# The seven-product form carried into w_down, with partial sums added up in DRAM

## The chip, the cores and the metric

The kernel runs on one core of one Trainium2 chip. The metric is device time in microseconds (us) from launch to end. The kernel before has a median of 2252.35 us over 3 runs (2251.71 to 2253.55). Everything is float32 at the input and output.

## What is computed

One layer of an encoder over 512 tokens and a model width of 2048: a norm, a combined projection into two groups of heads (dilated window attention and gated linear attention), an output projection with a residual, and then the part that matters here, a gated feed-forward block with a hidden width of 5632, and a last norm:

```python
h = rmsnorm(x, ffn_norm_w[l])
x = x + (jax.nn.silu(h @ w_gate[l]) * (h @ w_up[l])) @ w_down[l]
return rmsnorm(x, final_norm_w)
```

The change touches the last product, `@ w_down`: a 512 x 5632 matrix (called g below) times a 5632 x 2048 one, and what comes just before and after it.

## The kernel before, in words

**Precision.** Every large product is made of three matmuls. Each operand is split into a high part `hi` (rounded to the matmul type fp32r, a cast on ACT) and a low part `lo` (the rest, a subtraction on VectorE, DVE), and hi x hi, hi x lo and lo x hi are summed in PSUM.

**Memory.** There are 70 slots of [128, 512] called `a` (`s2`), 16 slots of [128, 1024] called `b` (`s4`) and the 8 PSUM banks `ps`. A slot given back goes to the end of a queue of free slots and is reused in that order; whoever writes it next waits for its last reader.

**Order.** The program is written in the order in which each engine executes: each engine takes its instructions in program order, and so do the queues of SP and POOL, from which transfers are issued. Work that should run beside matmuls is put between them by hand: `urgent` holds generators of which `run_urgent` executes one step at a time.

**w_gate and w_up** (`Feed`, lines 1059 to 1205). These already use a form with seven instead of eight block products for each pair of K-tiles (a K-tile is 128 rows of the contraction): both operands are cut into a 2 x 2 arrangement of blocks, sums of blocks are made on DVE, and seven products of 256 tokens are made. A piece is four K-tiles by 256 columns: a 512 KB load, `sums` (lines 1095 to 1097, DVE), `split` (1107 casts on ACT, 1112 subtractions on DVE), `products` (1137 to 1139, 42 matmuls of 256 columns). In turn i the program has the split of piece i+1 and the sums of piece i+2, then the products of piece i. After four pieces `evac` takes the sums out of PSUM, and every second time the gated result goes to DRAM as a tile `gd[j]` (line 1180), 256 hidden columns for all tokens. The operands made from x for this form come from `pair_operands` (lines 974 to 988).

**w_down** (lines 1209 to 1283). The 44 K-tiles of g are worked in three groups of K-tiles, 0 to 17, 18 to 35, 36 to 39, and a tail, 40 to 43. `g_load` and `g_split` bring g back from `gd` and split it. In each group, for each of four blocks c of 512 output columns, a job (`run_job`) goes through the K-tiles: for each, one half of a 512 KB load of w_down is split (`st.split`, lines 196 and 197), three halves ahead, and 4 x 3 matmuls of 512 columns follow (lines 293 to 295), one PSUM bank for each block of 128 tokens. At the end of a job `evac_down` adds the four banks, scaled by the row factor `rstd2`, to the residual tiles `x1` (line 1247), which POOL's queue has loaded from `xd` in DRAM at the end of w_up (line 1244).

**The tail** (`finish`, from line 1292). It goes token block by token block: for each of four blocks of 512 columns 12 matmuls (lines 1325 to 1327), the residual, the squares for the norm on ACT, a product with the norm's weight on DVE (line 1331). After the four blocks, `later` works out the factor of the last norm, scales (line 1311) and stores. The 16 halves of weights that the tail needs are split during the jobs of the third group, because there the lookahead grows by `4 * j.tail + i`.

Of the kernel before, what the change touches and what calls it, by code (L numbers as in the profile page):

```python
# [117 lines left out]
def layer(nc, tc, x, attn_norm_w, w_in, rel_table, gw_f, gb_f, gw_b, gb_b, gla_norm_w, w_out,  # L118
# [7 lines left out]
    with tc.manual_schedule(), \  # L126
# [136 lines left out]
        def run_job(j):  # L263
            if j.start:
                j.start()
            if j.limit:
                st.limit = j.limit
            banks = [ps.get() for _ in range(4)]
            per = len(j.kts) // j.n
            for i in range(j.n):  # L270
                if j.before:
                    j.before(i)
                st.load()
                st.split(j.first + i + AHEAD + (4 * j.tail + i if hasattr(j, "tail") else 0))
                _, _, wh, wl = st.halves[j.first + i]
                ks = j.kts[i * per:(i + 1) * per]
                for b in range(4):
                    for s_, k in enumerate(ks):
                        xh, xl = j.acts(k)
                        first = i == 0 and s_ == 0  # L280
                        last = i == j.n - 1 and s_ == per - 1
                        if j.kind == "A":
                            o = banks[b].t
                            c = slice(b * P, (b + 1) * P)
                            mm(o, wh.t[:, c], xh.t, start=first, stop=False)  # L285
                            mm(o, wh.t[:, c], xl.t, start=False, stop=False)  # L286
                            mm(o, wl.t[:, c], xh.t, start=False, stop=last)  # L287
                        else:
                            n = 512 // per
                            o = banks[b].t[:, 0:n]  # L290
                            c = slice(b * P, (b + 1) * P)
                            w = slice(s_ * n, (s_ + 1) * n)
                            mm(o, xh.t[:, c], wh.t[:, w], start=first, stop=False)  # L293
                            mm(o, xh.t[:, c], wl.t[:, w], start=False, stop=False)  # L294
                            mm(o, xl.t[:, c], wh.t[:, w], start=False, stop=last)  # L295
# [760 lines left out]
        n_out = len(jobs) - 1  # L1056


        class Feed:

            def __init__(self):
                self.units = [(w, j) for j in range(FF // 256) for w in (w_gate, w_up)]
                self.per = NP // 2
                self.seq = [(u, q) for u in range(len(self.units)) for q in range(self.per)]
                self.seq.insert(self.per + 1, self.seq.pop(self.per - 1))
                self.n = len(self.seq)
                self.raw, self.S, self.sets = {}, {}, {}  # L1070
                self.n_load = self.n_sums = 0

            def load(self):
                while self.n_load < self.n and len(self.raw) < 3 and s4.free:
                    u, q = self.seq[self.n_load]
                    w, j = self.units[u]
                    k = 4 * q
                    r = s4.get(F32, [P, 2, 4, P])
                    sp.dma_start(out=r.t.rearrange("p a b c -> p (a b c)").rearrange("p (k c) -> p k c", k=4),
                                 in_=w[k * P:(k + 4) * P, j * 256:(j + 1) * 256].rearrange("(k p) c -> p k c", p=P))  # L1080
                    self.raw[self.n_load] = r
                    self.n_load += 1

            def sums(self, i):


                if i != self.n_sums or i >= self.n:
                    return
                self.n_sums += 1
                if i not in self.raw:  # L1090
                    self.load()
                r = self.raw[i].t
                S = self.S[i] = s4.get(F32, [P, 2, 4, P])
                s_ = S.t
                dve.tensor_tensor(s_[:, :, 0:2], r[:, :, 1:3], r[:, :, 0:1].to_broadcast([P, 2, 2, P]), op=OP.add)  # L1095
                dve.tensor_tensor(s_[:, :, 2], s_[:, :, 0], r[:, :, 2], op=OP.add)
                dve.tensor_tensor(s_[:, :, 3], s_[:, :, 2], r[:, :, 3], op=OP.add)

            def split(self, i):
                if i >= self.n or i in self.sets:  # L1100
                    return
                r = self.raw[i]
                parts = [(r.t[:, :, 1:4], [P, 2, 3, P]), (self.S[i].t, [P, 2, 4, P])]
                his = []
                for src, shape in parts:
                    hi = s4.get(F32R, shape)
                    act.copy(hi.t, src)  # L1107
                    his.append(hi)
                out_ = []
                for (src, shape), hi in zip(parts, his):  # L1110
                    lo = s4.get(F32R, shape)
                    dve.tensor_tensor(lo.t, src, hi.f, op=OP.subtract)  # L1112
# [3 lines left out]
                self.load()  # L1116

            def products(self, i, banks):
                st_ = self.sets.pop(i)
# [109 lines left out]
        def down_start(q):  # L1229
            if q == 0:  # L1230
                g_load(0)
            if q == 1:
                st.until = None
                st.limit = 3
                st.load()
                g_load(1)
            if q == 2:
                g_split(0)
                st.split(down_first + 2)
            if q == 3:  # L1240
                for c in range(4):
                    x1[c] = [s2.get() for _ in range(4)]
                    for t in range(4):
                        pool.dma_start(out=x1[c][t].t, in_=xd[4 * c + t])

        def residual(c, t, bank):
            dve.scalar_tensor_tensor(x1[c][t].t, bank.t, rstd2[:, t:t + 1], x1[c][t].t, op0=OP.mult, op1=OP.add)  # L1247
# [8 lines left out]
        def before_down(h0, c, more):  # L1256
            def f(i):
                k = h0 + i
                if c == 0 and k % 2 == 0:
                    g_load(k // 2 + 2)  # L1260
                    g_split(k // 2 + 1)
                if more == LAST and c == 1 and i == 0:
                    g_split(FF // 256 - 1)
            return f

        def drop_g(k):
            put(*gT.pop(k))

        LAST = 40
        state["g"] = 0  # L1270
        st.until = len(st.pieces)
        down_first = len(st.halves)
        h0 = 0
        for h1 in (18, 36, LAST):
            for c in range(4):
                j = job("B", [piece512(w_down, c * 512, k) for k in range(h0, h1, 2)], list(range(h0, h1)),
                        lambda k: gT[k], evac_down(c), rate=1.0, before=before_down(h0, c, h1))
                if c == 3:
                    j.drop = drop_g
                if h1 == LAST:  # L1280
                    j.tail = c
            h0 = h1

        wf = []

# [8 lines left out]
        def finish():  # L1294

            first = len(st.halves)
            st.big = first
# [17 lines left out]
            def run():  # L1315
                for t in range(4):
                    ys = []
                    for c in range(4):
                        b = ps.get()
                        tok = slice(t * P, (t + 1) * P)  # L1320
                        for k in range(per):
                            st.split(first + c * per + k + 1)
                            _, _, wh, wl = st.halves[first + c * per + k]
                            xh, xl = gT[LAST + k]
                            mm(b.t, xh.t[:, tok], wh.t, start=k == 0, stop=False)  # L1325
                            mm(b.t, xh.t[:, tok], wl.t, start=False, stop=False)  # L1326
                            mm(b.t, xl.t[:, tok], wh.t, start=False, stop=k == per - 1)  # L1327
# [8 lines left out]

        run_last = finish()
        for n, j in enumerate(jobs):
            if getattr(j, "tail", None) == 0:
                start_tail()  # L1340
            run_job(j)
            if n == n_out:
                ff.run()
        drain()
        run_last()


# [25 lines left out]
```

## Time and profile before

| | |
|---|---|
| median of 3 runs | 2252.35 us |
| the profiled execution | 2252.81 us, of which the span from the first to the last instruction is 2251.0 |
| granted TensorE clock | 0.998 of full speed |
| TensorE busy | 2231.6 us, 99% |
| VectorE busy | 1453.2 us, 65% |
| ScalarE (ACT) busy | 900.2 us, 40% |
| data moved by transfers | 274 MB, 122 GB/s |

The page of the profile gives busy time by engine, the same in 40 slices of the span, the chain of work that ended last, and groups of instructions by line. In a group, `out<-in` names tiles without buffer numbers, then come the shapes, the count, the busy time in us, the mean of one in ns, and the idle time before them with what ended it. In a timeline the columns are the start, the length in us, the engine, the line and the operation, and in brackets the idle time of the engine before it and what released it. A matmul's length in the profile overlaps that of its neighbours, so two matmuls' distance is read from their starts. PE is TensorE, PEld its weight loads, SPq and POOLq the queues on which transfers are issued.

### The profile page before, as it was taken

What the parts mean: (1) busy time and instruction counts of PE and PEld (TensorE: products, weight loads), DVE (VectorE), ACT (ScalarE), POOL (GpSimd) and SP (SyncE); (2) the same over time, 40 slices, a digit from 0 to 9 for tenths busy, and PEclk for the clock granted to TensorE, in tenths of its full rate; (3) what the DMA queues carried; (4) which work ended last, traced back from release to release, by engine and by line L of the source; (5) the groups of instructions that cost most, each with busy time, mean ns of one, the idle gap of its engine ahead of it and who ended that gap; (6) DMA issues with size and microseconds to landing.
All of it is one profiled execution on the core that took longest, in us unless ns stands there. A gap on an engine that the chain in (4) does not pass through costs nothing.

```text
span 2251.0 us, 33982 instructions
## 1 busy us (share of the span) xinstructions
PE 2231.6 (99%) x13662; PEld 2001.6 (89%) x13662; DVE 1453.2 (65%) x2429; ACT 900.2 (40%) x1505; POOL 40.4 (2%) x79
## 2 busy tenths in 40 slices
PE   8999999999999999999999999999999999999998
PEld 7888887888888888999999999999999888888886
DVE  4366665744454356888888888888888623332356
ACT  5244454443454344433444344443444422322332
POOL 0000000000000100000000000000000100000000
PEclk9999999999999999999999999999999999999999
DMA  5524624332323432333333333433334942343312
GB/s 204 157 83 137 191 80 130 91 115 64 103 71 127 140 122 75 113 123 118 116 122 113 121 117 116 126 114 113 122 114 136 340 151 86 123 166 100 116 38 75
DMA packets 193358, 274.02 MB, mean 122 GB/s; under 512 B 13327, under 2 KB 129215, under 8 KB 193200
## 3 DMA queue, kind: packets, MB, share of 16 engines
q1 hardware_dynamic: 187584, 256.22, 36.2%
q0 software_dynamic: 4720, 14.58, 1.8%
q8 instruction: 107, 1.75, 0.3%
q10 hardware_dynamic: 896, 1.06, 0.1%
q14 instruction: 51, 0.42, 0.1%
HBM read 239.24 MB, written 19.99 MB: 115 GB/s over the span
## 4 chain that ended last, share of the span: by engine, by line
PE 97%; DVE 1%; ACT 1%; DMA 0%; issue 0%; ACTq 0%; SPq 0%
PE ps L1139 13%; PE ps L1137 13%; PE ps L1138 13%; PE ps L293 12%; PE ps L295 12%; PE ps L294 12%; PE ps L285 5%; PE ps L286 5%; PE ps L287 5%; PE ps L514 1%; PE ps L841 1%; PE ps L1326 1%; PE ps L1325 1%; PE ps L1327 1%; PE ps L554 1%; PE ps L553 1%
## 5 line engine op out<-in xcount | busy, mean ns | idle before, releaser
L1139 PE MATMUL ps<-a,b 128*128 128x256 f32 x2464 | 698.4, 283 | 2.9 <-DVE b L1112 2.9
L1137 PE MATMUL ps<-a,b 128*128 128x256 f32 x2464 | 698.1, 283 | 0.0
L1138 PE MATMUL ps<-a,b 128*128 128x256 f32 x2464 | 698.0, 283 | 0.0
L1107 ACT CAST b<-b 128x768 fp32r<-128x768 f32 x352 | 326.8, 942 | 406.5 <-DVE b L1112 253.5
L1139 PEld LDWEIGHTS ps<-a,b 128*128 128x128 f32 x2464 | 473.8, 192 | 3.8 <-DVE b L1112 3.8
L1138 PEld LDWEIGHTS ps<-a,b 128*128 128x128 f32 x2464 | 473.8, 192 | 0.0
L1137 PEld LDWEIGHTS ps<-a,b 128*128 128x128 f32 x2464 | 473.7, 192 | 0.0
L197 DVE TENSOR_TENSOR a<-b,a 128x512 fp32r<-128x512 f32 x420 | 279.5, 688 | 253.3 <-ACT a L196 253.1
L1112 DVE TENSOR_TENSOR b<-b,b 128x768 fp32r<-128x768 f32 x352 | 373.1, 1089 | 102.2 <-PE ps L1138 63.6
L293 PE MATMUL ps<-a,a 128*128 128x512 f32 x976 | 382.7, 392 | 0.0
L295 PE MATMUL ps<-a,a 128*128 128x512 f32 x976 | 380.0, 389 | 0.0
L294 PE MATMUL ps<-a,a 128*128 128x512 f32 x976 | 380.0, 389 | 0.0
L196 ACT CAST a<-b 128x512 fp32r<-128x512 f32 x420 | 249.2, 619 | 264.9 <-PE ps L295 239.5
L295 PEld LDWEIGHTS ps<-a,a 128*128 128x128 f32 x976 | 183.2, 188 | 38.5
L294 PEld LDWEIGHTS ps<-a,a 128*128 128x128 f32 x976 | 183.3, 188 | 37.2
L293 PEld LDWEIGHTS ps<-a,a 128*128 128x128 f32 x976 | 183.3, 188 | 37.1
L285 PE MATMUL ps<-a,a 128*128 128x512 f32 x416 | 167.8, 403 | 0.0
L286 PE MATMUL ps<-a,a 128*128 128x512 f32 x416 | 163.0, 392 | 0.0
L287 PE MATMUL ps<-a,a 128*128 128x512 f32 x416 | 162.7, 391 | 0.0
L1095 DVE TENSOR_TENSOR b<-b 128x512 f32<-128x512 f32 x176 | 120.4, 684 | 4.1 <-DMA b<-in_w_up_dram 4.1
L1247 DVE SCALAR_TENSOR_TENSOR a<-ps,small,a 128x512 f32<-128x512 f32 x64 | 45.5, 750 | 118.6 <-PE ps L295 107.5
L578 ACT CAST b<-ps 128x512 fp32r<-128x512 f32 x64 | 37.6, 587 | 144.8 <-PE ps L514 142.9
(196 smaller groups left out, 2312.1 us busy)
## 6 DMA issues: line engine op xcount, KB each, us to landing
b<-in_w_gate_dram SPq DMA_DIRECT2D x88, 512.0 KB, 3.5
b<-in_w_up_dram SPq DMA_DIRECT2D x88, 512.0 KB, 3.5
b<-in_w_down_dram SPq DMA_DIRECT2D x88, 512.0 KB, 4.9
b<-in_w_in_dram SPq DMA_DIRECT2D x96, 256.0 KB, 4.3
b<-in_w_in_dram SPq DMA_DIRECT2D x48, 512.0 KB, 4.1
b<-in_w_out_dram SPq DMA_DIRECT2D x32, 512.0 KB, 4.5
a<-a SPq DMA_DIRECT2D x96, 128.0 KB, 2.3
gd<-b SPq DMA_DIRECT2D x22, 512.0 KB, 2.7
```

Of the source, the lines that this page charges most:

```text
L197: dve.tensor_tensor(h[3].t, r, h[2].f, op=OP.subtract)
L285: mm(o, wh.t[:, c], xh.t, start=first, stop=False)
L286: mm(o, wh.t[:, c], xl.t, start=False, stop=False)
L287: mm(o, wl.t[:, c], xh.t, start=False, stop=last)
L293: mm(o, xh.t[:, c], wh.t[:, w], start=first, stop=False)
L294: mm(o, xh.t[:, c], wl.t[:, w], start=False, stop=False)
L295: mm(o, xl.t[:, c], wh.t[:, w], start=False, stop=last)
L1107: act.copy(hi.t, src)
L1112: dve.tensor_tensor(lo.t, src, hi.f, op=OP.subtract)
L1137: mm(o, wh, xh, start=head, stop=False, skip_group_check=True)
L1138: mm(o, wh, xl, start=False, stop=False, skip_group_check=True)
L1139: mm(o, wl, xh, start=False, stop=end, skip_group_check=True)
```

## The change

Of the 22 pairs of K-tiles in w_down, pairs 2 to 19 go over to the seven-product form. Pairs 0 and 1 stay plain and are worked first, pairs 20 and 21 remain the tail.

- `Feed` is divided: what loads, sums up and splits the weights goes into a class `Blocks`, from which `Feed` and a new class `Down` inherit. For w_gate and w_up nothing changes.
- `Down` works in three chunks of six pairs. In each chunk, for each block c of 512 columns, it goes through the six pairs: one 512 KB piece of w_down, its sums and splits, and seven products. Each product goes into a PSUM bank of its own, in two halves of 128 tokens, with the tokens' side as the stationary operand: 42 matmuls of 256 columns.
- `operands` is a generator that brings a pair of g back from `gd`, makes the sums and the splits, in four steps a pair; it waits for 2 free b slots and for 13 free a slots. `make(n)` executes n steps: two at the end of w_up, three before each K-tile of the plain jobs, two after each piece of `Down`.
- After the six pairs of a chunk the seven banks are copied to SBUF by ACT and sent to `md` in DRAM: on SP in the first chunk, on POOL's queue and added to what is there (`accum_op`) in the second and third. Four of the seven are copied within the last piece, three at the start of the next (`evac_late`).
- In the last chunk, `combine(c)` reads the seven sums and the residual tiles back and puts the result of a block together on DVE, seven sums and four scaled additions, spread over later pieces as `urgent` work. For the last block it is executed in the tail, before the first use of that block.
- The plain jobs no longer add to `x1`: ACT scales the bank, and POOL's queue adds it to `xd` in DRAM. `x1` is loaded by `combine`.
- The weights of the tail are split two halves at a time in the last four pieces, eight of the 16; the others in the tail, each just before its matmuls. The tail's other work is as before.

```diff
@@ run_job
-                st.split(j.first + i + AHEAD + (4 * j.tail + i if hasattr(j, "tail") else 0))
+                st.split(j.first + i + AHEAD)
@@ plain jobs
         def evac_down(c):
             def f(banks):
                 for t in range(4):
-                    residual(c, t, banks[t])
+                    y = s2.get()
+                    act.activation(y.t, banks[t].t, AF.Copy, scale=rstd2[:, t:t + 1])
+                    put(banks[t])
+                    pool.dma_start(out=xd[4 * c + t], in_=y.t, accum_op=OP.add)
+                    put(y)
             return f
+        def before_down(c):
             def f(i):
+                if c == 0 and i == 0:
+                    g_split(1)
+                dn.make(3)
+                if c == 3:
+                    dn.load()
+                    if i >= 1:
+                        dn.sums(i - 1)
+                    if i == 2:
+                        dn.split(0)
             return f
@@ class Down(Blocks)
+            def operands(self):
+                a, z = slice(0, 256), slice(256, 512)
+                tt = dve.tensor_tensor
+                for q in [q for ch in self.chunks for q in ch]:
+                    while len(s4.free) < 2:
+                        yield
+                    r = s4.get(F32, [P, 2, 512])
+                    sp.dma_start(out=r.t.rearrange("p f t -> p (f t)"), in_=gd[q])
+                    yield
+                    while len(s2.free) < 9 + 4:
+                        yield
+                    n1, f2 = r.t[:, 1], r.t[:, 0]
+                    t13, t24 = s2.get(), s2.get()
+                    tt(t13.t[:, a], n1[:, z], n1[:, a], op=OP.subtract)
+                    tt(t13.t[:, z], f2[:, z], n1[:, z], op=OP.add)
+                    tt(t24.t[:, a], f2[:, z], t13.t[:, a], op=OP.add)
+                    tt(t24.t[:, z], t24.t[:, a], f2[:, a], op=OP.subtract)
+                    yield
...
+                    for i, (src, hi, lo, hf) in enumerate(todo):
+                        if i == 0:
+                            act.activation(hi, src, AF.Copy, scale=-1.0)
+                            dve.scalar_tensor_tensor(lo, src, -1.0, hf, op0=OP.mult, op1=OP.subtract)
+                        else:
+                            act.copy(hi, src)
+                            tt(lo, src, hf, op=OP.subtract)
+                        if i:
+                            put((r, t13, t24)[i - 1])
+                        if i % 2:
+                            yield
...
+            def products(self, i):
...
+                prods = [(R(0), "B11"), (R(2), "B21"), (Z(2), "T2"), (Z(1), "T1"), (Z(0), "T3"), (Z(3), "B22"),
+                         (R(1), "T4")]
+                for n, ((wh, wl), x) in enumerate(prods):
...
+                    for h in range(2):
+                        o = self.banks[n].t[:, h * 256:(h + 1) * 256]
+                        t = slice(h * P, (h + 1) * P)
+                        mm(o, xh[:, t], wh, start=first and h == 0, stop=False, skip_group_check=True)
+                        mm(o, xh[:, t], wl, start=False, stop=False, skip_group_check=True)
+                        mm(o, xl[:, t], wh, start=False, stop=last, skip_group_check=True)
+                    if last:
+                        if n < 4:
+                            self.evac(ch, c, n, self.banks[n])
+                        else:
+                            self.late.append((ch, c, n, self.banks[n]))
...
+            def combine(self, c):
+                m = [s2.get(F32, [P, 2, 256]) for _ in range(7)]
+                for n in range(7):
+                    sp.dma_start(out=m[n].t.rearrange("p s c -> p (s c)"), in_=md[7 * c + n])
+                x1[c] = [s2.get() for _ in range(4)]
+                for t in range(4):
+                    pool.dma_start(out=x1[c][t].t, in_=xd[4 * c + t])
+                yield
+                yield
...
+            def run(self):
+                for i, (ch, c, q) in enumerate(self.seq):
+                    self.load()
+                    self.sums(i)
+                    self.split(i)
+                    self.sums(i + 1)
+                    self.sums(i + 2)
+                    self.split(i + 1)
+                    self.evac_late()
+                    while q not in self.x:
+                        self.make(1)
+                    self.products(i)
+                    self.make(2)
+                    run_urgent()
+                    if ch == len(self.chunks) - 1 and c == 3:
+                        n = self.chunks[ch].index(q)
+                        if n == 0:
+                            g_load(FF // 256 - 2)
+                        if n == 1:
+                            g_split(FF // 256 - 2)
+                            g_load(FF // 256 - 1)
+                            st.until, st.limit = None, 1
+                            start_tail()
+                        if n == 2:
+                            g_split(FF // 256 - 1)
+                        if n >= 2:
+                            st.load()
+                            st.split(tail_first + 2 * (n - 1))
+                self.evac_late()
+                st.limit, st.big = 3, tail_first
+                drain()
@@ finish, in the tail
+                        if t == 0 and c == 3:
+                            for _ in dn.done:
+                                pass
                         residual(c, t, b)
```

More of the change, by code (lines that the diff above doesn't have):

```diff
@@ L1240, in down_start @@
             if q == 3:
[L1241 to L1244, printed above, removed]
+                dn.make(2)
         def residual(c, t, bank):
@@ L1272, in layer @@
         down_first = len(st.halves)
[L1273 to L1282, printed above, removed]
+        for c in range(4):
+            j = job("B", [piece512(w_down, c * 512, k) for k in (0, 2)], list(range(4)),
+                    lambda k: gT[k], evac_down(c), before=before_down(c))
+            if c == 3:
+                j.drop = drop_g
+        down_pieces = len(st.pieces)
+        tail_first = len(st.halves)
+        dn = Down([list(range(2, 8)), list(range(8, 14)), list(range(14, 20))])
         wf = []
@@ L1343, in layer @@
                 ff.run()
-        drain()
+        dn.run()
         run_last()
```

129 lines of the change are left out of this document (102 added, 27 removed).

## The prediction

> **What bounds the kernel now.** First the page: the busy shares, the slices and the chain that ended last.
>
> ```profile
> span 2251.0 us, 33982 instructions
> PE 2231.6 (99%) x13662; PEld 2001.6 (89%) x13662; DVE 1453.2 (65%) x2429; ACT 900.2 (40%) x1505; POOL 40.4 (2%) x79
> ...
> DVE 4366665744454356888888888888888623332356
> ...
> PE 97%; DVE 1%; ACT 1%; DMA 0%; issue 0%; ACTq 0%; SPq 0%
> ```
>
> TensorE is busy all the time and is the chain. VectorE is not the limit, but in the slices of w_gate/w_up it is eight tenths full, and in w_down (from slice 32 on) two to three tenths. The windows of these two stages:
>
> ```profile
> 1300.00:1700.00 400.00, 400.00 (x3336) 400.00 (x3335) 349.54 (x527) 163.16 (x188) 0.00 (x0) 1.00 0.38 119
> 1800.00:1900.00 100.00, 100.00 (x443) 82.81 (x442) 30.31 (x45) 23.09 (x37) 0.00 (x0) 1.00 0.39 131
> ```
>
> Columns: length, PE, weight loads, DVE, ACT, POOL, clock, DMA share, GB/s. The first stage already runs the seven-product form, with DVE at 349.5/400 = 87%; the second is plain. So w_down has room on DVE, and only fewer or shorter matmuls can shorten it. What one matmul costs must come from start to start in the timeline, since the durations of 283 and 390 ns in the groups overlap. First and last of 52 successive rows of the seven-product stage, then first and last of 77 rows of w_down:
>
> ```profile
> 1399.81 0.28 PE L1138 MATMUL ps<-a,b 128*128 128x256 f32 x1
> ...
> 1405.93 0.28 PE L1138 MATMUL ps<-a,b 128*128 128x256 f32 x1
> ```
>
> ```profile
> 1829.69 0.39 PE L295 MATMUL ps<-a,a 128*128 128x512 f32 x1
> ...
> 1846.92 0.39 PE L293 MATMUL ps<-a,a 128*128 128x512 f32 x1
> ```
>
> 6.12/51 = 0.120 us at 256 columns, 17.23/76 = 0.2267 us at 512: twice 256 costs 6% more than one 512.
>
> **The change, step by step.**
>
> *1. Matmuls.* A pair of K-tiles for 512 columns was 4 token blocks x 2 K-tiles x 3 = 24 matmuls, 24 x 0.2267 = 5.44 us. It becomes 7 products x 2 token halves x 3 = 42 of 256 columns, 42 x 0.120 = 5.04 us. 18 pairs x 4 column chunks = 72 pieces: 72 x 0.40 = **-28.8 us** on the path.
>
> The Trainium skill (TensorE: Matmul & The Clock Gate, Back-to-back issue gap) speaks against the change: it gives sustained pacings of about 81 ns at 128 columns and 131 at 512. On a line between them a 256 would take 98 ns, 42 of them 4.10 us against 3.14 for 24 long ones, and the 72 pieces would cost +69 us. The trace has 120 and 226.7 ns in long unbroken rows, so it disagrees, and the sum goes by the trace.
>
> *2. DVE in the pieces.* Each piece now needs the column sums of the weights and two splits, as in w_gate/w_up, and each pair its operands from gd (four half-width sums, four splits). One piece without extras, and one set of operands:
>
> ```profile
> 878.42 0.42 DVE L974 TENSOR_TENSOR a<-a 128x256 f32<-128x256 f32 x1
> ...
> 881.95 2.42 DVE L974 TENSOR_TENSOR a<-a,a 128x256 fp32r<-128x256 f32 x4 [1.98 <-ACT a L988]
> 884.29 0.69 DVE L1095 TENSOR_TENSOR b<-b 128x512 f32<-128x512 f32 x1
> ...
> 887.82 0.42 DVE L974 TENSOR_TENSOR a<-a 128x256 f32<-128x256 f32 x1
> ...
> 888.94 2.57 DVE L974 TENSOR_TENSOR a<-a,a 128x256 f32<-128x256 f32 x5
> 891.42 0.69 DVE L1095 TENSOR_TENSOR b<-b 128x512 f32<-128x512 f32 x1
> ...
> 894.95 0.68 DVE L1095 TENSOR_TENSOR b<-b 128x512 f32<-128x512 f32 x1
> ...
> 898.47 0.69 DVE L1095 TENSOR_TENSOR b<-b 128x512 f32<-128x512 f32 x1
> ```
>
> A piece is 898.47 - 894.95 = 3.52 us; a set of operands 891.42 - 887.82 = 3.6 us, or 884.29 - 878.42 = 5.87 where DVE waited for ACT. The piece alone is covered by 5.04 us of PE. By the 70 a-slots (7 for each pair's operands, 13 free wanted before a set is begun) I count eight sets made in the plain jobs and ten in the seven-product part, in two runs of 12 and 8 pieces around the changes of chunk, half a set in each piece: 3.52 + 1.8 = 5.32, over PE by 0.28. DVE has a lead:
>
> ```profile
> 1399.84 2.10 DVE L1112 TENSOR_TENSOR b<-b,b 128x768 fp32r<-128x768 f32 x2 [1.04 <-PE ps L1138]
> ```
>
> It splits the next piece as soon as PE releases the buffers and is through after 2.1 of 5.04 us, so 2.9 us are in hand. 12 x 0.28 = 3.4 exceeds that by 0.5, 8 x 0.28 = 2.2 does not. I take +1; bounds 0 and, with 5.87 us a set, 20 x (3.52 + 2.94 - 5.04) - 2 x 2.9 = +23.
>
> *3. The plain start.* K-tiles 0 to 3 stay plain: 16 halves of 12 x 0.2267 = 2.72 us. Ahead of each half's split stand three steps of the operand maker, on ACT and DVE, which work in order. DVE's other work there, and the state it starts in:
>
> ```profile
> 1757.93 1.29 DVE L1174 TENSOR_TENSOR b<-b,a 128x512 f32<-128x512 f32 x2
> 1764.14 0.69 DVE L1222 SCALAR_TENSOR_TENSOR a<-b,a 128x512 fp32r<-128x512 f32 x1 [4.92 <-ACT a L1221]
> ...
> 1765.36 0.68 DVE L197 TENSOR_TENSOR a<-b,a 128x512 fp32r<-128x512 f32 x1
> 1765.96 0.42 DVE L1148 TENSOR_TENSOR b<-ps,a 128x256 f32<-128x256 f32 x1
> 1766.29 0.41 DVE L1156 TENSOR_TENSOR a<-a,ps 128x256 f32<-128x256 f32 x1
> ...
> 1767.22 0.68 DVE L1148 TENSOR_TENSOR a<-ps,a 128x512 f32<-128x512 f32 x1
> 1767.94 1.02 DVE L1148 TENSOR_TENSOR b<-ps,a 128x256 f32<-128x256 f32 x2
> ...
> 1770.68 1.22 DVE L1178 TENSOR_TENSOR b<-b,b 128x1024 f32<-128x1024 f32 x1
> ```
>
> ```profile
> L1137 PE MATMUL ps<-a,b x2464: 278/283/415, 867.5 to 1762.2; 128*128 128x256 f32 x190
> ```
>
> PE starts the last of these short matmuls at 1762.2, and DVE is through with what goes before at about 1759.2, 3 us ahead. Seven sets come before the split of half 10: 7 x 3.6 = 25.2; nine halves at 0.60 (1765.36 to 1765.96) 5.4; one pair of the plain gated tiles 1.2; the last unit's evacuation 0.42 + 0.41 + 0.68 + 1.02 + 1.22 = 3.7. Sum 35.5, less the 3 ahead: 32.5 us after PE begins. PE wants half 10 at 10 x 2.72 = 27.2: 5.3 us late. Further, SP's store of that unit waits for the multiplication at the end of the evacuation, and the next load of gd stands behind it on SP; the operand maker uses it at once. How long such transfers take:
>
> ```profile
> b<-in_w_down_dram SPq DMA_DIRECT2D x88, 512.0 KB, 4.9
> ...
> b<-gd SPq DMA_DIRECT2D x22, 512.0 KB, 6.2
> ...
> xd<-a POOLq DMA_DIRECT2D x16, 256.0 KB, 2.6
> a<-xd POOLq DMA_DIRECT2D x16, 256.0 KB, 6.9
> ```
>
> About 4.5 us less the 1.2 us of splits between: +3.3. Together **+8.5**; bounds 0 (the maker held back by buffers) and 13 (6.2 us to land, a second such wait). The 16 loads of x1 that were issued here move to the last chunk; nothing waits for them in either place.
>
> *4. Evacuations, accumulates, combine.* Each chunk and column block ends with seven copies on ACT and seven 256 KB stores to md, the first chunk on SP, the others as accumulates on POOL's queue; the plain jobs add 16 to xd. A copy from PSUM:
>
> ```profile
> L578 ACT CAST b<-ps 128x512 fp32r<-128x512 f32 x64 | 37.6, 587 | 144.8 <-PE ps L514 142.9
> ```
>
> At 0.6 us, 84 + 16 of them on an ACT that is 41% busy (163/400, above) are hidden. Four of the seven are copied during the last piece, three behind the next piece's casts, some 4 us into it, before the sixth bank is wanted again: nothing. No accumulate is in the trace: its landing lies between a store, 2.6, and a store plus a load, 2.6 + 6.9 = 9.5 us; I take two stores, 5.2. In the last chunk SP reads md back, so it waits for these accumulates, and behind that stand the next weight loads; DVE comes to the first sum two pieces later, 10.1 + 2.1 = 12 us into the piece, and can be 1.5 us late. Issue 4 + landing + 4 to load gives 13.2 with 5.2, so 0 to +4 for the first block; the second and third blocks' combines begin a piece or two later and wait for nothing. I take +1. DVE's 11 operations for a block (7 us over seven pieces) fit: 3.52 + 1.0.
>
> By the Trainium skill (DMA: Bandwidth & Descriptors, Anatomy of one DMA), a POOL transfer takes 2.0 us plus bytes over 436 GB/s, 2.6 us for 256 KB; the store's row agrees. Its rules for authors say that an accumulate reads its destination and writes it later; two passes would be an estimated 5.2 us. No run here shows one yet.
>
> *5. The last pieces.* In the last six, DVE also splits the two last gated pairs and the first tail weights, whose load is issued in the same step that uses it, behind seven reads of md: a wait of 0 to 4 us, partly covered. +1.5.
>
> *6. The tail.* All 16 halves of the last four K-tiles were split ahead (the lookahead grew by 4 a block); now eight are. The other eight stand behind the residuals of the first token block, on DVE in order.
>
> ```profile
> 2206.16 0.75 DVE L1247 SCALAR_TENSOR_TENSOR a<-ps,small,a 128x512 f32<-128x512 f32 x1 [1.24 <-PE ps L1327]
> 2206.94 0.69 DVE L1331 TENSOR_TENSOR a<-a,a 128x512 f32<-128x512 f32 x1
> 2208.88 0.75 DVE L1247 SCALAR_TENSOR_TENSOR a<-ps,small,a 128x512 f32<-128x512 f32 x1 [1.24 <-PE ps L1327]
> ...
> 2213.63 0.75 DVE L1247 SCALAR_TENSOR_TENSOR a<-ps,small,a 128x512 f32<-128x512 f32 x1
> ...
> 2215.03 0.74 DVE L1247 SCALAR_TENSOR_TENSOR a<-ps,small,a 128x512 f32<-128x512 f32 x1
> ...
> 2241.52 0.75 DVE L1247 SCALAR_TENSOR_TENSOR a<-ps,small,a 128x512 f32<-128x512 f32 x1 [1.24 <-PE ps L1327]
> ```
>
> ```profile
> 2207.48 0.19 ACT L394 ACTIVATION_READ_ACCUMULATOR a<-a 128x1 f32 x1
> ```
>
> Groups end 2.72 apart. The third block's first weights are ready only after the second block's residual (0.78), its square on ACT (2206.94 to 2207.67, 0.73), a cast (0.6) and the split (0.6): 2.7 us, and the fourth block's alike: PE ends some 5.2 us late. Then the fourth block's combine, all at once: 15.4 us into the tail, 11 operations at 0.65, to 22.5. From there DVE needs 4.75 for the last group of a token block (2208.88 to 2213.63) and 1.40 for each other (2213.63 to 2215.03): 4.75 + 2 x (3 x 1.40 + 4.75) + 3 x 1.40 = 26.9, so the last residual starts at 49.4; PE's last group allows it at 48.8. It was at 43.6 (2241.52; the tail's 16 groups of 2.72 begin at 2197.9), and 9.5 us follow, as before. **+5.8**; bounds 4 and 9 (accumulates at 9.5 us delay the combine).
>
> Sum: -28.8 + 1 + 8.5 + 1 + 1.5 + 5.8 = -11.0. The profiled execution took 2252.8 us (1.8 more than its span), 0.5 over the median, which is nothing here: 2252.8 - 11 = 2242.
>
> **Rivals.**
> (a) *The covers hold*: the maker is slowed by its buffers and the plain start loses at most 2 us, the rest of the sum as it is or smaller: 2242 - 6.5 = 2235, and down to 2229 if steps 2, 4 and 5 cost nothing and the tail 4. For it: DVE has 70% free in w_down now. Against: the maker's steps stand ahead of the split in DVE's order.
> (b) *Accumulates at the upper price*: +3 in the first combine, +3 in the tail: 2248, within no change of before.
> (c) *Slower: the operand makers wait.* Ten sets are made while DVE is nearly full, each a chain of load, sums on DVE, casts on ACT, splits on DVE, and the second row of step 2's fence shows such a wait, 1.98 us. With it in each, step 2 costs +23 instead of 1: 2264. It decides from where the 11 us are eaten: 20 x (0.28 + w) - 5.8 = 12, w = 0.61 us a piece, 1.2 us a set. Against it: the second set of that fence did not wait, and a piece lies between the load and the first sum.
>
> **How the numbers follow.** A measurement of this kernel can tell about 0.2%, 4.5 us. Forecast 0.50 (2236 to 2248: faster 0.45, same 0.05); (a) 0.12, faster; (b) 0.13 (same 0.10, faster 0.03); (c) 0.25, 2250 to 2268 (slower 0.22, same 0.03). Faster 0.60, same 0.18, slower 0.22. The range 2230 to 2262 leaves out a tenth above and the end of (a) below.
>
> **What would show it.** Step 1: rows of 42 matmuls 0.120 us apart, each with its start at 5.04 from the last piece's. Step 3: idle of some 8 us before the plain matmuls, ended by the splits of DVE, and one DVE wait for gd. Step 2: PE idle ended by DVE's split near the changes of chunk. Step 4: a landing time for md's accumulates and DVE waits for md. Step 6: PE idle of 2.6 us twice in the tail, DVE without gaps behind the combine, last residual 49 us into the tail. Wrong would make it: idle spread over all 72 pieces; matmuls over 0.120; weight loads late behind md.

## The result, and the profile after

The changed kernel takes 2269.8 us (median of 4 runs, 2268.95 to 2271.63) against 2252.83 for the kernel before beside it: a ratio of 1.0077, 95% interval 1.0059 to 1.0094. It is slower by 0.8%, where 2242, some 0.5% faster, was forecast, and 2269.8 lies above the range of 2230 to 2262.

The page of the changed kernel: busy shares, slices, POOL's queue, the chain, and the landing of md's accumulates.

```profile
span 2267.8 us, 37302 instructions
PE 2216.3 (98%) x14958; PEld 2046.6 (90%) x14958; DVE 1648.7 (73%) x2749; ACT 1011.5 (45%) x1641; POOL 104.4 (5%) x151
...
DVE 4366665744454456888888888888888777978677
...
q0 software_dynamic: 15088, 33.45, 6.9%
...
PE 79%; issue 12%; DMA 3%; DVE 3%; POOL 1%; ACT 1%; SPq 0%; POOLq 0%; ACTq 0%; DVEq 0%
...
md<-a POOLq DMA_DIRECT2D x56, 256.0 KB, 8.7
```

The chain is no longer TensorE alone: transfers, DVE, POOL and ACT stand in it. The waits of TensorE name them (engine, line, releaser, us, times, longest):

```profile
PE ps L1362 <- ACT b L1101: 9.8, 1, 9.8
PE ps L294 <- DVE a L197: 9.0, 3, 6.6
PE ps L1363 <- DVE b L1106: 7.9, 7, 3.6
PE ps L1515 <- ACT b L196: 4.8, 2, 2.7
```

L294 are the plain jobs, L1362 and L1363 the seven-product pieces, L1515 the tail. The matmuls themselves do what step 1 said. First and last of 61 successive rows:

```profile
1849.75 0.28 PE L1364 MATMUL ps<-b,a 128*128 128x256 f32 x1
...
1856.95 0.28 PE L1364 MATMUL ps<-b,a 128*128 128x256 f32 x1
```

7.20/60 = 0.120 us. So the 28.8 us were gained and given back. How much where is read from the timeline of TensorE: for every matmul, the distance to the next start less 0.120 us (256 columns) or 0.2267 us (512), added up by stage. This counts idle time and slow matmuls alike.

| stage | lost, us | step of the prediction and its value |
|---|---|---|
| plain jobs, 1762 to 1810 | 14.0 | 3: 8.5 |
| pieces up to 2140 | 7.0 | 2 and 4: 2 |
| last pieces, to 2203 | 16.0 | 5: 1.5 |
| tail, matmuls | 9.4 | 6: 5.8 |

The sum is 46.4; less 28.8 that is +17.6, and the span grew by 16.8. The four rows of waits shown above make 31.5 us of it; most of the rest is matmuls at half speed. Around the longest pause of the plain jobs:

```profile
1776.85 0.39 PE L293 MATMUL ps<-a,a 128*128 128x512 f32 x1
1783.84 0.79 PE L294 MATMUL ps<-a,a 128*128 128x512 f32 x1 [6.60 <-DVE a L197]
...
1784.86 0.63 PE L293 MATMUL ps<-a,a 128*128 128x512 f32 x1
1785.28 0.63 PE L294 MATMUL ps<-a,a 128*128 128x512 f32 x1
...
1787.42 0.44 PE L293 MATMUL ps<-a,a 128*128 128x512 f32 x1
1787.70 0.40 PE L294 MATMUL ps<-a,a 128*128 128x512 f32 x1
```

After 6.6 us of idle time the matmuls come 0.42 us apart (the first 0.59), for 3.6 us (1783.84 to 1787.42), then 0.23 again after one step of 0.28. The windows show it as the granted clock (the column before the DMA share):

```profile
1762.00:1800.00 38.00, 28.48 (x108) 21.98 (x107) 30.34 (x64) 21.61 (x43) 6.92 (x8) 0.87 0.70 225
...
1850.00:1900.00 50.00, 50.00 (x419) 50.00 (x418) 35.25 (x50) 23.34 (x30) 0.00 (x0) 1.00 0.46 159
...
2150.00:2200.00 50.00, 36.82 (x286) 35.91 (x285) 35.72 (x53) 20.82 (x31) 10.58 (x15) 0.86 0.80 251
```

The Trainium skill (TensorE: Matmul & The Clock Gate, What's actually happening) says that the array runs at half clock until it has been busy for about 3.4 us; the 3.6 us here agree.

**Why the plain jobs wait.** SP's queue in the changed kernel, then the first sum of each of two sets of the operand maker on DVE:

```profile
1757.50 0.47 SPq L1307 DMA_DIRECT2D b<-gd  x1
1775.33 0.32 SPq L1190 DMA_DIRECT2D gd<-b  x1
1775.75 0.38 SPq L1307 DMA_DIRECT2D b<-gd  x1
1776.22 0.49 SPq L181 DMA_DIRECT2D b<-in_w_down_dram  x1
1776.81 1.69 SPq L1307 DMA_DIRECT2D b<-gd  x1
```

```profile
1781.63 0.43 DVE L1313 TENSOR_TENSOR a<-b 128x256 f32<-128x256 f32 x1 [5.12 <-DMA b<-gd]
...
1788.83 0.43 DVE L1313 TENSOR_TENSOR a<-b 128x256 f32<-128x256 f32 x1 [2.30 <-DMA b<-gd]
```

SP waits with the store of the last gated unit until DVE has made it (1775.33), and then issues what has gathered behind it at once. The first load of gd needs 5.9 us (1775.75 to 1781.63), the second 12.0 (1776.81 to 1788.83). Two rows of what SP's queue waited for in the whole run (line, releaser, us, times, longest), this store (the longest of its waits, 17.3 us) and the reads of md:

```profile
SPq L1190 <- DVE b L1188: 89.1, 22, 17.3
...
SPq L1401 <- DMA md<-a: 38.2, 21, 7.7
```

**Why the pieces of the third chunk wait.** In the first of the three blocks that are combined beside the pieces, seven reads of md hold SP for 15.6 us, up to 2109.3, and DVE then waits for the weights behind them:

```profile
2093.65 15.62 SPq L1401 DMA_DIRECT2D a<-md  x7
```

```profile
2114.66 0.69 DVE L1089 TENSOR_TENSOR b<-b 128x512 f32<-128x512 f32 x1 [5.38 <-DMA b<-in_w_down_dram]
```

TensorE's wait of 3.6 us follows from it, and with the half-speed matmuls behind it 5.4 of the 7.0 us.

**Why the last pieces wait.** SP's queue again, then ACT:

```profile
2133.60 11.59 SPq L1401 DMA_DIRECT2D a<-md  x7
2145.29 14.50 SPq L1073 DMA_DIRECT2D b<-in_w_down_dram  x5
2164.62 0.34 SPq L1223 DMA_DIRECT2D b<-gd  x1
2170.07 0.37 SPq L1073 DMA_DIRECT2D b<-in_w_down_dram  x1
2171.20 0.34 SPq L1223 DMA_DIRECT2D b<-gd  x1
2172.33 7.07 SPq L1401 DMA_DIRECT2D a<-md  x7
2181.43 19.77 SPq L181 DMA_DIRECT2D b<-in_w_down_dram  x8
```

```profile
2181.39 0.63 ACT L1231 ACTIVATE a<-b 128x512 fp32r<-128x512 f32 x1 [5.85 <-DMA b<-gd]
...
2189.17 1.14 ACT L196 CAST a<-b 128x512 fp32r<-128x512 f32 x2 [6.64 <-DMA b<-in_w_down_dram]
```

Seven reads of md hold SP for 11.6 us in the second block, of which it waited 8.0 us for accumulates. In the third block they hold it for 7.1 us, and there little of that is the accumulates. What SP waited for from 2172 to 2182 us:

```profile
SPq L1401 <- DMA md<-a: 2.8, 3, 1.2
SPq L181 <- DMA b<-gd: 2.0, 1, 2.0
SPq L1401 <- DMA b<-in_w_down_dram: 1.7, 1, 1.7
```

The last gated pair stands ahead of these reads; issued at 2171.20, it lands 10.2 us later; the first tail weights leave only at 2181.43 and arrive at 2189.1. ACT and DVE, in order, stand before them with the split of the next piece behind, and TensorE is idle for 9.8 us.

### The profile page after: what moved, and what is told of

The parts are those of the page before. It is cut to its first block, busy times and chain, and to the rows that moved or that the text cites. A ratio compares the mean times of both kernels' runs of the same rounds, so it can differ in the third digit from the quotient of the medians.

```text
span 2267.8 us, 37302 instructions
## 1 busy us (share of the span) xinstructions
PE 2216.3 (98%) x14958; PEld 2046.6 (90%) x14958; DVE 1648.7 (73%) x2749; ACT 1011.5 (45%) x1641; POOL 104.4 (5%) x151
## 3 DMA queue, kind: packets, MB, share of 16 engines
q0 software_dynamic: 15088, 33.45, 6.9%
## 4 chain that ended last, share of the span: by engine, by line
PE 79%; issue 12%; DMA 3%; DVE 3%; POOL 1%; ACT 1%; SPq 0%; POOLq 0%; ACTq 0%; DVEq 0%
PE ps L1149 13%; PE ps L1148 13%; PE ps L1147 13%; PE ps L294 5%; PE ps L293 5%; PE ps L295 5%; PE ps L285 5%; PE ps L286 5%; PE ps L287 5%; PE ps L514 1%; POOL md L1384 1%; DMA b<-gd 1%; DMA md<-a 1%; PE ps L841 1%; PE ps L1516 1%
## 5 line engine op out<-in xcount | busy, mean ns | idle before, releaser
L1101 ACT CAST b<-b 128x768 fp32r<-128x768 f32 x496 | 459.8, 942 | 539.4 <-DVE b L1106 381.2
L1106 DVE TENSOR_TENSOR b<-b,b 128x768 fp32r<-128x768 f32 x496 | 523.8, 1088 | 137.1 <-PE ps L1148 62.0
L1362 PE MATMUL ps<-b,a 128*128 128x256 f32 x1008 | 287.0, 285 | 9.8 <-ACT b L1101 9.8
L1363 PE MATMUL ps<-b,a 128*128 128x256 f32 x1008 | 287.5, 285 | 7.9 <-DVE b L1106 7.9
L1364 PE MATMUL ps<-b,a 128*128 128x256 f32 x1008 | 286.6, 284 | 0.0
L197 DVE TENSOR_TENSOR a<-b,a 128x512 fp32r<-128x512 f32 x280 | 187.2, 687 | 131.6 <-ACT a L196 127.8
L1362 PEld LDWEIGHTS ps<-b,a 128*128 128x128 f32 x1008 | 194.7, 193 | 10.0 <-ACT b L1101 10.0
L1363 PEld LDWEIGHTS ps<-b,a 128*128 128x128 f32 x1008 | 194.7, 193 | 9.5 <-DVE b L1106 9.5
L1364 PEld LDWEIGHTS ps<-b,a 128*128 128x128 f32 x1008 | 194.7, 193 | 0.0
L196 ACT CAST a<-b 128x512 fp32r<-128x512 f32 x280 | 164.5, 617 | 45.1 <-DMA b<-in_w_in_dram 17.9
L1089 DVE TENSOR_TENSOR b<-b 128x512 f32<-128x512 f32 x248 | 169.8, 685 | 19.9 <-DMA b<-in_w_down_dram 15.8
L285 PE MATMUL ps<-a,a 128*128 128x512 f32 x416 | 167.9, 404 | 0.0
L294 PE MATMUL ps<-a,a 128*128 128x512 f32 x400 | 157.8, 394 | 9.0 <-DVE a L197 9.0
L286 PE MATMUL ps<-a,a 128*128 128x512 f32 x416 | 163.0, 392 | 0.0
L287 PE MATMUL ps<-a,a 128*128 128x512 f32 x416 | 163.0, 392 | 0.0
L293 PE MATMUL ps<-a,a 128*128 128x512 f32 x400 | 160.1, 400 | 0.5 <-ACT a L196 0.5
```

The costliest lines, as they stand in the source:

```text
L1362: mm(o, xh[:, t], wh, start=first and h == 0, stop=False, skip_group_check=True)
L1363: mm(o, xh[:, t], wl, start=False, stop=False, skip_group_check=True)
L1364: mm(o, xl[:, t], wh, start=False, stop=last, skip_group_check=True)
```

## The experiments

e9 and e13 were run four times, the others once. Four runs of one kernel spread over up to 3.0 us, so gains of that size rest on the traces beside them.

The theory after the result: four separate places, with two causes in common. (A) The accumulates to md are slow, and SP, which waits for them, holds up weight loads. (B) In the plain jobs it is the store of the last unit that holds SP. The rivals were that the transfer engines are simply full, so that no order helps, and that DVE has too much to do.

**e1: plain stores.** The output then lacks the sums over the chunks.

```diff
-                    pool.dma_start(out=md[7 * c + n], in_=y.t, accum_op=OP.add)
+                    pool.dma_start(out=md[7 * c + n], in_=y.t)
```

> The 56 transfers to md of the second and third chunk are plain stores; their sums over the chunks are left out. Theory A (the accumulates, with 8.7 us to land and about twice the transfer time of a store, hold up SP's reads of md, and the weight loads behind them on SP, in the third chunk and in the last pieces): most of the 9 us lost between 2045 and 2181 us and at least half of the 14 us lost in the last pieces go, 2270 -> 2253 to 2260; the landing of md falls to about 3 us. Theory B (it is the place of the loads in SP's queue and the number of bytes in the last chunk, whatever the stores are): 2265 to 2270, with TensorE still idle about 9 us before the last pieces.

Measured: 2258.24 us, 11.6 less. The loss in the pieces up to 2140 falls from 7.0 to 0, that in the last pieces from 16.0 to 10.1. The landing times of transfers that touch md, in the changed kernel and then in this one:

```profile
  DMA to landing us min/median/max: 2.0/7.9/13.6
```

```profile
  DMA to landing us min/median/max: 2.1/3.6/10.3
```

That is theory A for the third chunk. In the last pieces less than the half asked for went: the pause there is 6.0 us instead of 9.8, and the seven reads of md hold SP for 6.9 us even with plain stores.

**e2: md read on POOL's queue.**

```diff
-                    sp.dma_start(out=m[n].t.rearrange("p s c -> p (s c)"), in_=md[7 * c + n])
+                    pool.dma_start(out=m[n].t.rearrange("p s c -> p (s c)"), in_=md[7 * c + n])
```

> The 28 reads of md go out on POOL's queue instead of SP's, so that no weight load stands behind them. If the order on SP's queue is the cause (A1), the waits of DVE for w_down pieces in the third chunk go and the time falls by 5 to 15 us, 2255 to 2265. If the transfer engines themselves are full there (A2), the weight loads are as late as before and the time stays within 4 us of 2270.

Measured: 2257.70 us, 12.1 less. SP's weight loads of the third chunk now run in one unbroken group:

```profile
2089.20 65.17 SPq L1073 DMA_DIRECT2D b<-in_w_down_dram  x14
```

Lost up to 2140: 2.2 instead of 7.0; in the last pieces 8.3 instead of 16.0. The accumulates are still there, as slow as before (the page's median for md<-a is 8.7 in both). So for the third chunk it is the order on SP (A1), not the engines' load; in the last pieces half of the loss stays.

**e11: both together.** The edits of e1 and e2; the sums over the chunks are left out.

> The changed kernel with md's accumulates as plain stores (the sums over the chunks are left out) and with md read on POOL's queue. Each alone took 12 us away. If both act through the same chain (an accumulate lands late, SP waits for it, the weight loads behind it are late), together they take little more than one: 2254 to 2258. If they are two causes, transfer time and order in the queue, together they take 18 to 24: 2246 to 2252.

Measured: 2254.88 us, 14.9 less, where the two alone gave 11.6 and 12.1. It lies in the range of one shared chain: most of a slow accumulate's harm comes through SP, which waits for it.

**e3: the maker behind the splits.**

```diff
-                dn.make(3)
...
                 st.split(j.first + i + AHEAD)
+                if j.after:
+                    j.after()          # dn.make(2) in the plain jobs
```

> In the plain jobs the operand maker takes two steps a K-tile instead of three, and stands behind the split of the weights instead of ahead of it. By step 3 of the prediction (the maker ahead of the splits, on DVE in order, and its waits for gd) the 14 us lost between 1762 and 1795 us fall to 0 to 4, so 2270 -> 2256 to 2260, unless sets that are missing later cost it again. If the loss there came from somewhere else (the copies that scale the banks, the accumulates to xd), it stays: 2268 to 2272.

Measured: 2269.67 us, no change, in the range expected if the loss came from somewhere else. It did, but not from the copies or the accumulates to xd that were named there. The short pauses are gone, and one wait on DVE took their place:

```profile
1784.79 0.43 DVE L1315 TENSOR_TENSOR a<-b 128x256 f32<-128x256 f32 x1 [10.94 <-DMA b<-gd]
```

A load of gd, issued at 1774.24 behind the same store, needs 10.5 us, and TensorE waits 8.7 us at once. The plain jobs lost 10.9 us instead of 14.0, and 2.2 came back in the first pieces. The maker's place is not what costs most there; the load is.

**e8: the last unit's store on POOL.**

```diff
-                    sp.dma_start(out=gd[j], in_=c)
+                    (pool if j == FF // 256 - 1 else sp).dma_start(out=gd[j], in_=c)
```

> The store of the last gated unit goes out on POOL's queue instead of SP's; the maker's order and steps are as in the changed kernel. If SP, held by this store for 17 us, and the burst of eight loads behind it are the cause of the two waits for gd (5.1 and 2.3 us), these waits go, the 6.6 us pause falls to 2 us or less, no half-speed matmuls follow, and the loss of 14 us in the plain jobs falls to about 5: 2260 to 2263. If the maker's work ahead of the splits is enough by itself, as step 3's 5.3 us say, 3 to 6 us of it stay; if all of the 14 stay, the store is not the cause.

Measured: 2261.77 us, 8.0 less. The plain jobs lose 5.8 us instead of 14.0. SP is free, and the loads of gd leave when the maker asks for them:

```profile
1758.81 0.94 SPq L1307 DMA_DIRECT2D b<-gd  x2
1759.85 0.60 SPq L181 DMA_DIRECT2D b<-in_w_down_dram  x1
1762.99 0.32 SPq L1307 DMA_DIRECT2D b<-gd  x1
```

The 5.8 us that stay are pauses of 1.4, 1.4, 1.1 and 0.3 us before L294 and some slower matmuls beside them. They are the maker's work ahead of the splits: step 3 had 5.3 us for it.

**e4: the last loads earlier.**

```diff
+                    if ch == len(self.chunks) - 1 and c == 2 and q == self.chunks[ch][-1]:
+                        g_load(FF // 256 - 2)
                     if ch == len(self.chunks) - 1 and c == 3:
                         n = self.chunks[ch].index(q)
                         if n == 0:
-                            g_load(FF // 256 - 2)
-                        if n == 1:
                             g_split(FF // 256 - 2)
                             g_load(FF // 256 - 1)
-                            st.until, st.limit = None, 1
                             start_tail()
-                        if n == 2:
+                        if n == 1:
                             g_split(FF // 256 - 1)
+                            st.until, st.limit = None, 1
+                            st.load()
```

> The loads of the two last gated pairs, of the first tail weights and of the norm's weight are issued one or two pieces earlier, ahead of the reads of md for the third block. If the 14 us in the last pieces come from these loads standing behind those reads and being used at once, they fall to 0 to 5 and the time to 2256 to 2261. If they come from full transfer engines whatever the order, the pause only moves to another piece: 2266 to 2271.

Measured: 2264.09 us, 5.7 less, between the two expectations. The last pieces lose 8.6 us instead of 16.0, and the tail a little more. The gated pair and the first tail weights now leave ahead of md's reads, but the second pair of tail weights is still behind them and leaves at 2184.87:

```profile
2172.80 0.37 SPq L181 DMA_DIRECT2D b<-in_w_down_dram  x1
2173.26 8.25 SPq L1401 DMA_DIRECT2D a<-md  x7
2184.87 2.93 SPq L181 DMA_DIRECT2D b<-in_w_down_dram  x4
```

Order is a part of it. The rest is put down to full transfer engines (around 400 GB/s from 2176 to 2192 us): the first tail weights, issued at 2172.80, kept ACT waiting for 5.4 us, until 2184.8. The last gated pair lands 10.2 us after its issue in the changed kernel, 9.4 in e1, 10.5 in e2 and 10.4 here, so neither the kind of store nor the order on SP changes that; before, the two pairs took 3.4 in the median. No run takes these loads off the engines, so this last cause is argued, not shown.

**e5: the tail's weights split before the tail.**

```diff
                 st.limit, st.big = 3, tail_first
+                st.split(tail_first + 16)
                 drain()
```

> All 16 halves of the tail's weights are split before the tail begins, eight of them as the last thing before it. By step 6 the two pauses of TensorE in the tail (2.8 and 2.3 us, and the half-speed matmuls behind them, 9.4 us together) go; the combine of the last block still holds DVE. 2270 -> 2262 to 2266. If DVE is the bound in the tail by its backlog behind the combine alone, TensorE's pauses go without a change of the time: 2268 to 2271.

Measured: 2267.04 us, 2.8 less. This lies between the two expectations, and both mechanisms are there. TensorE loses nothing in the tail any more (0 instead of 9.4 us), but the end hardly moves, because DVE is late. The last residual in the changed kernel and here:

```profile
2258.28 0.75 DVE L1254 SCALAR_TENSOR_TENSOR a<-ps,small,a 128x512 f32<-128x512 f32 x1 [1.24 <-PE ps L1517]
```

```profile
2255.77 0.74 DVE L1254 SCALAR_TENSOR_TENSOR a<-ps,small,a 128x512 f32<-128x512 f32 x1
```

There DVE had waited for TensorE; here it has not (no bracket), and TensorE's last matmul had started at 2249.1, 6.7 us before. The last residual comes 50.0 us into the tail, where step 6 had 49.4. The pauses had hidden a backlog on DVE behind the combine of the fourth block.

**e9: all five mended.** The edits of e2, e3, e4, e5 and e8, and half of the last scaling on ACT:

```diff
-                    if t == 3 and c % 2:
+                    if c % 2:
                         act.activation(o.t, o.t, AF.Copy, scale=rstdf[:, t:t + 1])
```

> All together: the last gated unit's store on POOL, the maker behind the splits with two steps, md read on POOL's queue, the last loads earlier, the tail's weights split before the tail, and half of the last scaling on ACT instead of DVE. If the four places are separate and each has the cause named, TensorE's time is left with little beside its 450 us of matmuls after w_up: 2270 - 14 - 9 - 12 - 8 = 2227, and I expect 2225 to 2237. If they share a cause that is not removed (too many bytes at the end), 2245 to 2260.

Measured: 2235.94 us (2235.17 to 2238.18), ratio to the kernel before 0.9929, interval 0.9912 to 0.9945. This lies within the range expected of four separate places. What is left of TensorE's waits in w_down:

```profile
PE ps L1365 <- DVE b L1109: 5.4, 6, 2.0
...
PE ps L1364 <- ACT b L1104: 0.5, 1, 0.5
```

The loss counted as in the table is 9.5 us instead of 46.4, none of it in the plain jobs or the tail; 5.5 us are in the last pieces.

**e10: the same, with the maker's old place.** As e9 without the edit of e3.

> As the run before, but with the maker's three steps ahead of the splits as in the changed kernel. The difference to the run before is what that order costs alone: by step 3's sum without the wait for gd about 5 us; if SP's store was all of it, within 1 us.

Measured: 2238.63 us, 2.7 more than e9's median and between the two expectations; e9's own runs reach 2238.18. The traces differ by more than that: TensorE loses 5.5 us in the plain jobs, as step 3's sum without the wait said, and e9, which loses nothing there, gives 2.4 of it back in the first pieces.

**e12: all mended, plain stores.** e9 with e1's edit; the sums over the chunks are left out.

> The kernel with everything mended (2235.9), with md's accumulates as plain stores (the sums over the chunks are left out). What is left of the accumulates' price where nothing stands behind them on SP: if only the order mattered, 2234 to 2237; if their transfer time still delays the loads of the last chunk (TensorE lost 5.5 us there between 2150 and 2170 us), 2228 to 2233.

Measured: 2237.07 us against 2235.94, just above the range for order alone and within e9's own runs (up to 2238.18). Accumulates that nothing on SP waits behind cost nothing that can be seen.

**e13: the last scaling of three token blocks on ACT.** e9, with its last edit as

```diff
-                    if t == 3 and c % 2:
+                    if t < 3 or c % 2:
```

> The kernel with everything mended, and the last scaling of the first three token blocks wholly on ACT. In its tail DVE runs without a gap from 2179 us to the end, so DVE is the bound there: 0.4 us less for each of the six operations taken from it, 2232.5 to 2235. If TensorE's end is the bound, no change: 2235 to 2237.

Measured: 2233.16 us (2232.7 to 2235.55), ratio to the kernel before 0.9918, interval 0.9901 to 0.9935. DVE was the bound in the mended tail: the span ends 12.6 us after the start of TensorE's last matmul in e9, 9.8 here and 9.9 in the kernel before. This version beats both kernels: 19 us below the one before, 37 below the changed one.

## Why the prediction failed, by its own steps

The step that failed most is step 5, put at 1.5 us and measured at 16.0; steps 3, 4 and 6 were too small as well.

**Bound and step 1: right.** 72 pieces of 42 matmuls at 0.120 us; the mended kernels show that the gain is there to be had. The line through the pacings of the Trainium skill (TensorE: Matmul & The Clock Gate, Back-to-back issue gap), which would have made this stage 69 us longer, is refuted by the 61 rows above.

**Step 2: right in size.** It took +1, and the short pauses around 2050 to 2075 us, behind a 2.7 us wait of the maker for gd, are 1.7 us in all; nothing else was lost where operands are made in the pieces. Rival (c), which put the slower case there, is not what happened: the waits for gd that cost most (5.1 and 2.3 us) are in the plain jobs.

**Step 3: right mechanism, mis-sized.** The store holding SP, the load behind it and the work ahead of the splits are all there. The maker's own 5.3 us measured 5.5 to 5.8 (e10, e8). The wait was put at 3.3 us, from a landing time of 4.5, less than the 6.2 of gd's own row in the same fence; two loads took 5.9 and 12.0, since a queue held for 17 us lets go of everything at once. And a term was missing: half-speed matmuls behind the pause.

**Step 4: right mechanism, a mis-sized term.** The accumulates were put at 5.2 us; they take 8.7 in the median, near the upper bound of 9.5. The working for the first block (13.2 against 12 + 1.5) stood or fell with that figure: with 8.7 it is 3.2 us too late, and TensorE waited 3.6 and lost 5.4 around 2113. That later blocks "wait for nothing" was wrong for SP.

**Step 5: the failed step, and half of the miss** (14.5 of the 27.8 us between -11.0 and +16.8)**.** It said "a wait of 0 to 4 us, partly covered" and measured 16.0. It did see the order, loads behind seven reads of md and used at once, but priced them as lone transfers on a free queue. The last gated pair took 10.2 us to land; the first tail weights left 10.2 us after it, behind the seven reads (7.1 us) and a wait of 2.0 us for this pair, and took another 7.7. e1, e2 and e4 each take 6 to 8 us of this away; that full engines are the rest is argued (e4).

**Step 6: half right.** The two pauses, put at 5.2 us, measured 5.1 (2.8 and 2.3); the half-speed matmuls behind them, 4.3 us with two short waits on DVE, were not thought of. DVE's backlog is real (e5), but in the changed kernel TensorE was late enough to cover it. The last residual came 53.1 us into the tail instead of 49.4.

**Rivals.** (a) asked for a plain start that the maker does not slow; it cost 5.5 us even without the wait. (b), accumulates at the upper price, was the right cause with the wrong reach: +3 in the first block and +3 in the tail, while in the first two blocks they acted through SP on everything behind the reads. What was summed as small separate terms met in one place, the 18 us from 2171 us on:

```profile
DMA  9999999999999999999999999999999999972000
```

This is the busy share of the transfer engines in 40 slices from 2170 to 2195 us: accumulates, seven reads of md, x1, the norm's weight, the last gated pair and the tail's weights, all at once.

## What to carry to other kernels

A queue that issues in order is as slow as the slowest thing it waits for: keep reads that wait for a slow producer off the queue that feeds the engine in the chain, and put a store that waits for late work on a queue where nothing urgent follows (12.1 and 8.0 us here). A load used in the step that issues it is priced with all that stands before it on its queue and on the engines, not with its median. And in the changed kernel each pause of TensorE of 2 us or more cost another 1.5 to 2 us in slow matmuls, whatever its length, so several small waits add up to more than their sum.

## What was not expected of the hardware

- An accumulating transfer of 256 KB lands after 8.7 us in the median; POOL's queue took 6.9% of 16 engines' 2267.8 us for 33.45 MB, before 1.8% of 2251.0 us for 14.58 MB. The 72 accumulates are the difference: (156.5 - 40.5)/72 = 1.6 us of all engines each, against 0.73 us for 256 KB of the plain ones. With stores in place of md's accumulates (e1) the same bytes took 4.7%, and these stores landed after 3.5 us.
- Behind a pause of 6.6 us TensorE ran at half speed for 3.6 us. Waits of 2.7 and 2.1 us in the tail brought it too (4.3 us lost beside them); pauses of 1.4 us in e8 did not show it. Yet in the changed kernel pauses of 0.5 and 1.1 us close together, some 8 us after the long one, were followed by 3.3 us of it (1794.21 to 1797.50), so the length of a single pause does not settle it.
- Eight 512 KB loads, a store and four accumulates issued from 1774.7 to 1782 us kept the engines busy all the time (212 to 414 GB/s between 1776 and 1795 us), and a single load of gd among them took 12.0 us, where the median of its row before is 6.2.
